# Norm, weight bounds and copies between the first output projection and the first feed-forward stage

## The chip, the cores and the metric

The kernel runs on one core of a Trainium2 chip. The metric is the device time in microseconds, the median of several runs of the whole program. The engines are named as in the profile: PE (matrix engine), PEld (its weight loads), DVE (VectorE), ACT (ScalarE), POOL (GpSimd) and SP (the engine that issues most of the loads).

## The reference

Two layers of a hybrid backbone work on 1024 latent tokens and 256 context tokens with 1024 channels. What matters here is the seam between the mixer of layer 0 and its feed-forward part:

```python
        h_lat = h_lat + g1 * y_lat
        h_lat = h_lat + g2 * swiglu(modulate(rms_norm(h_lat, norm2_g[i]), sh2, sc2),
                                    ffn_w_gate[i], ffn_w_up[i], ffn_w_down[i])
        if not last:
            h_ctx = h_ctx + cg1 * y_ctx
            h_ctx = h_ctx + cg2 * swiglu(modulate(rms_norm(h_ctx, norm2_g[i]), csh2, csc2),
                                         ffn_w_gate[i], ffn_w_up[i], ffn_w_down[i])

def swiglu(u, w_gate, w_up, w_down):
    return (jax.nn.silu(u @ w_gate) * (u @ w_up)) @ w_down
```

`y_lat` and `y_ctx` are the mixer's outputs, already multiplied by `w_out`. The feed-forward width is 2816, that is 22 blocks of 128.

## The kernel before, in words

**Layout.** Channels lie on the 128 partitions, tokens along the free axis. The tokens are in three column pieces: 0 and 1 are the two latent halves of 512, piece 2 is the context (256). A matrix product in fp32 precision is made of three products: each operand is split into a high part (a cast on ACT) and a low part (a subtraction on DVE, `split`, line 302, its cast line 300). `lin` multiplies one block of 128 output channels by all eight input blocks: 24 matmuls for each piece.

**Output projection** (`out_proj`). Two groups run one after the other: pieces (2, 0), then piece 1. Each group has eight blocks. A block's weights are fetched one block ahead through two pairs of buffers. After a block's matmuls, DVE adds the result to the residual `h` (line 1210), ACT squares the new `h` (line 509) and DVE adds the squares to an accumulator (line 514). After each block the generator `fill` is stepped once. At the end of a group `after1` is called. For group one it writes `h` to DRAM (POOL), computes the RMS factors (`rms`: one-column matmuls of the accumulator against ones, a square root and a reciprocal, matmuls that spread the result over the partitions, a copy), makes the context's normalized operand `uf` (lines 556 to 559), loads `h` of piece 1, and makes the first operands of the Strassen-Winograd products (`wino_first`). For group two it writes `h` and computes the factor, which is kept in `rest`.

**Bounds of weights.** Operands of the later half-precision products need scales. `qkv_sums` (the `fill` generator) loads 44 tiles of later weights, half a megabyte each, on POOL's queue, and ACT sums their absolute values (`abs_sums`, line 1264). It yields after every third tile. The first four tiles belong to the first feed-forward scales and are needed by `first_scales(0)` in `after1`; the other 40 are needed much later.

**Feed-forward, first stage** (`ffn`, layer 0). A loop over 22 blocks computes the context's hidden part: load and split gate and up weights, 24 matmuls of each, SiLU on ACT (line 1542), a product on DVE (line 1543), a store on POOL. From the third block on, each block steps the generator `second` (`wino_second`), which makes 20 of the operands for the latent half (line 1365 and what follows, casts at line 1358); they are held behind the previous block's last split on DVE. Then the Winograd stage begins: for each pair i of hidden blocks, gate and up products (`wino_steps`, matmuls at line 1462), with copies of the accumulator out of PSUM (`snap`, line 1467) between products that go on in the same accumulator. `fetch` loads the weights of the next product ahead and, where they have no scale yet, sums their absolute values.

**Order.** The program is written in source order, and the framework orders each engine's queue by planned times; an instruction earlier in the source goes first where both are ready. Engines run their queues in order. `follow(ins)` adds an order edge: the instructions in its block that run on the engine of `ins` are queued behind it. It adds no semaphore. Buffers come from pools: 20 of 4 KB (`S4`: tiles for the bounds, staging of gate and up weights, operands), 34 of 2 KB (`S2`), and so on.

## Time and profile before

| | |
|---|---|
| median of 3 runs | 2901.01 us (2895.24 to 2902.95) |
| profiled execution: its own time, its span | 2897.71 us, 2895.6 us |
| mean granted PE clock | 0.978 |
| output projection on PE | 718.2 to 839.1 us |
| context blocks of the feed-forward stage on PE | 845.1 to 975.3 us |
| Winograd stage on PE, from | 975.4 us |

In the tables by stretch, "10.20, 7.72 (x27)" is the stretch's length, then PE's busy time in it and the number of instructions recorded; the clock is the share of full speed that was granted to PE. In the timelines a row gives start, duration, engine, line, operation, tiles and shapes; the bracket at its end is how long the engine had been idle before it and what ended that. The names of tiles are the kernel's: `ps` and `pq` are accumulators in PSUM, `tk` holds squares, `wh` and `wl` the two parts of weights, `ws` and `s` staging buffers.

### The profile page before, as it was taken

The page shows a single profiled execution, that of the slowest core. Times are in us where ns is not written, and L with a number is a line of the kernel's source. Part 1 is how long each engine was busy: PE and PEld are TensorE (multiplying, and loading weights), DVE is VectorE, ACT ScalarE, POOL GpSimd, SP SyncE. Part 2 cuts the span into 40 slices and gives each one's busy share as a digit, 9 for nine tenths or more (in the row PEclk, how much of TensorE's full clock was granted, in tenths as well). Part 3 has the DMA queues.
Part 4 walks back from the last instruction along what each step waited for, and adds up shares of the span by engine and source line. Part 5 has one row for each costly group of instructions (what it writes and reads, how often), then busy time and mean ns, then how long its engine had stood idle before and what let it go on. Part 6 is the DMA issues. An engine that isn't in the chain of part 4 may idle for free. (4 is left out here: it accounts for less than half of the span.)

```text
span 2895.6 us, 46377 instructions
## 1 busy us (share of the span) xinstructions
PE 2758.4 (95%) x16419; PEld 1688.7 (58%) x16419; DVE 2081.9 (72%) x3857; ACT 1620.2 (56%) x2857; POOL 593.0 (20%) x977
## 2 busy tenths in 40 slices
PE   6989999999989999999999999999999899999998
PEld 3766557878879644444555844666664444444554
DVE  4778867585467798877886777777775778775755
ACT  4664325453675666654555555666663567554543
POOL 1012013354220111123120012343321112112000
PEclk8989999999999999999999999999999999999999
DMA  7574435358785655566995698777864756425753
GB/s 257 191 275 161 159 124 159 109 165 293 279 342 177 211 209 196 201 221 219 315 336 193 238 330 333 167 170 167 177 186 166 248 199 246 151 95 184 237 190 117
DMA packets 323363, 607.60 MB, mean 210 GB/s; under 512 B 89910, under 2 KB 131576, under 8 KB 323130
## 3 DMA queue, kind: packets, MB, share of 16 engines
q1 hardware_dynamic: 254682, 387.53, 41.6%
q0 software_dynamic: 66144, 212.91, 20.8%
q10 hardware_dynamic: 2304, 4.20, 0.4%
q8 instruction: 129, 2.11, 0.3%
q14 instruction: 104, 0.85, 0.1%
HBM read 455.33 MB, written 135.53 MB: 204 GB/s over the span
## 5 line engine op out<-in xcount | busy, mean ns | idle before, releaser
L1462 PE MATMUL ps<-s,s 128*128 128x512 f16 x2244 | 507.3, 381 | 8.9 <-ACT g L1467 4.7
L1462 PEld LDWEIGHTS <-s 128*128 128x128 f16 x2640 | 258.7, 98 | 332.3 <-issue 26.8
L296 PE MATMUL ps<-s,wh 128*128 128x256 f32 (+3 forms) x1764 | 402.3, 331 | 12.1 <-ACT wh L300 5.7
L1231 ACT ACTIVATE s<-s,c 128x512 f16<-128x512 f32 (+1 forms) x324 | 233.2, 752 | 147.3 <-DMA s<-d 71.4
L1232 DVE SCALAR_TENSOR_TENSOR s<-s,c,s 128x512 f16<-128x512 f32 (+1 forms) x324 | 247.3, 792 | 87.0 <-ACT s L1231 85.9
L1679 PE MATMUL ps<-s 128*128 128x512 f16 (+2 forms) x1308 | 303.8, 378 | 2.3 <-DVE s L1232 2.0
L296 PE MATMUL pq<-s,wh 128*128 128x512 f16 (+1 forms) x988 | 271.4, 352 | 5.0 <-DMA wh<-d 3.0
L296 PE MATMUL ps<-s,wl 128*128 128x256 f32 (+3 forms) x882 | 264.4, 332 | 2.6 <-DMA wl<-d 1.6
L1679 PEld LDWEIGHTS <-s 128*128 128x128 f16 x1536 | 148.4, 98 | 179.5 <-issue 7.4
L296 PEld LDWEIGHTS <-wh 128*128 128x128 f16 x1664 | 159.1, 99 | 151.1 <-issue 12.2
L287 POOL DMA_DIRECT2D d<-s x201 | 108.6, 541 | 652.2 <-DVE s L1523 186.1
L348 ACT CAST mat<-cs 128x1024 fp32r<-128x1024 f16 (+2 forms) x120 | 111.5, 934 | 140.5 <-PE ps L296 53.5
L296 PEld LDWEIGHTS ps<-s,wh 128*128 128x128 f32 x1088 | 178.3, 193 | 18.4 <-ACT wh L300 5.9
L296 PE MATMUL ps<-s,mat 128*128 128x512 f32 x696 | 183.1, 410 | 3.1 <-DVE s L302 2.8
L1462 PE MATMUL ps<-s,wh 128*128 128x512 f16 x608 | 182.3, 379 | 1.6 <-DVE g L1476 1.2
L296 PE MATMUL pq<-s,wl 128*128 128x512 f16 (+1 forms) x494 | 171.2, 352 | 0.0
L296 PEld LDWEIGHTS <-s 128*128 128x128 f16 x2400 | 113.6, 98 | 80.7 <-issue 12.8
L296 PEld LDWEIGHTS ps<-s,mat 128*128 128x128 f32 x696 | 135.7, 197 | 37.1 <-DVE s L302 3.2
L1264 ACT ACTIVATE t<-s 128x1024 bf16<-128x1024 f32 (+1 forms) x164 | 141.5, 864 | 13.4 <-DVE c L483 8.6
L296 PE MATMUL sc<-s,s 128*128 128x65 f16 (+3 forms) x2688 | 142.6, 231 | 3.2 <-ACT t L2080 2.4
L296 PEld LDWEIGHTS <-wl 128*128 128x128 f16 x832 | 81.8, 99 | 81.2 <-DMA wl<-d 2.5
L1231 ACT ACTIVATE s<-t,c 128x512 f16<-128x512 f32 x172 | 115.2, 712 | 21.9 <-DVE c L1330 9.3
(435 smaller groups left out, 5505.9 us busy)
## 6 DMA issues: line engine op xcount, KB each, us to landing
s<-d SPq DMA_DIRECT2D x294, 256.0 KB, 4.2
d<-s POOLq DMA_DIRECT2D x157, 256.0 KB, 3.7
s<-in_down SPq DMA_DIRECT2D x154, 256.0 KB, 5.0
s<-in_ada_w POOLq DMA_DIRECT2D x48, 512.0 KB, 4.9
s<-in_gate SPq DMA_DIRECT2D x46, 512.0 KB, 4.0
s<-in_up SPq DMA_DIRECT2D x46, 512.0 KB, 3.8
d<-g POOLq DMA_DIRECT2D x87, 256.0 KB, 3.4
d<-tk POOLq DMA_DIRECT2D x82, 256.0 KB, 4.9
```

What stands on the lines that cost most here:

```text
L287: self.last_ldr = self.nc.gpsimd.dma_start(out, in_).ins
L296: return self.nc.tensor.matmul(o, l, r, start=st, stop=sp).ins
L348: self.nc.scalar.copy(m, st)
L1231: nc.scalar.activation(hi, src, AF.Copy, scale=scale)
L1232: nc.vector.scalar_tensor_tensor(lo, src, scale, hi, op0=MUL, op1=SUB)
L1264: self.nc.scalar.activation(junk[:, :t.shape[1]], t, AF.Abs, scale=2.0 ** -15, accum_out=st[:, k:k + 1])
L1462: nc.tensor.matmul(ps, x[:, sl], y, start=first and j == 0 and x is wh and y is xh, stop=j == 3 and x is wl, skip_group_check=True)
L1679: m = nc.tensor.matmul(acc[j][:, c0:c1], x[:, sl], y[:, xs], start=first and k == 0, stop=last and k == 2, skip_group_check=True)
```

## The change

Four things are edited.

1. In `out_proj` the norm of a group is no longer computed at its end. `after1` writes `h` and loads the next `h`; a new function `norm1` (RMS factors, `uf`, scales, `wino_first`) is called in the next group, after the matmuls of its first block.
2. The factor of the second group is computed inside a new generator `second1`, so at the first step of `second`, in the third block of the feed-forward stage.
3. `qkv_sums` yields after every tile. Group one steps it three times for each block, group two once, and `ffn` gets the same generator as `fill` and steps it once a block from the third block on, draining it after the loop. These steps and `second` follow both the last split on DVE and the last cast on ACT of the previous block.
4. In layer 0 the `fetch` of the second pair's gate weights comes behind the first five steps of the first gate product, and `abs_sums` queues its sums from there on behind the last copy out of PSUM (`last_snap`).

```diff
-    def out_proj(self, wname, y, groups, h, l, m, after, fill):
+    def out_proj(self, wname, y, groups, h, l, m, after, norm, fill):
...
-        for pcs in groups:
+        for g, pcs in enumerate(groups):
             for nb in range(KB):
                 wh, wl = ready.pop(0)
                 fetch()
                 acc = self.lin(wh, wl, 0, range(KB), y, pcs)
-                next(fill, None)
+                if g and nb == 0:
+                    norm(groups[g - 1])
+                for _ in range(1 if g else 3):
+                    next(fill, None)
...
     def abs_sums(self, tiles, st):
 
         junk = self.T(BF16, 1024)
-        for k, t in enumerate(tiles):
-            self.nc.scalar.activation(junk[:, :t.shape[1]], t, AF.Abs, scale=2.0 ** -15, accum_out=st[:, k:k + 1])
+        with self.follow(self.behind):
+            for k, t in enumerate(tiles):
+                self.nc.scalar.activation(junk[:, :t.shape[1]], t, AF.Abs, scale=2.0 ** -15,
+                                          accum_out=st[:, k:k + 1])
...
             self.abs_sums([t], self.qs[:, k:k + 1])
-            if j % 3 == 2:
-                yield
-        yield
+            yield
...
         def snap(ps, tile=tile):
             t = tile()
-            nc.scalar.copy(t, ps)
+            self.last_snap = nc.scalar.copy(t, ps).ins
             return t
...
-                lo = self.last_lo
+                lo, hi = self.last_lo, self.last_hi
...
                 if fb >= 2:
-                    with self.follow(last):
+                    with self.follow(last[0]), self.follow(last[1]):
                         next(second, None)
-                last = lo
+                        next(fill, None)
+                last = lo, hi
+            for _ in fill:
+                pass
...
-            fetch(i + 1, 0)
+            if i or begun:
+                fetch(i + 1, 0)
             for k in (3, 4, 5) if i == 0 and l == 1 else ():
                 g.to(k)
                 up.to(k)
             g.to(5)
+            if i == 0 and not begun:
+                self.behind = self.last_snap
+                fetch(1, 0)
             up.to(1)
...
-        rest = []
-
         def after1(pcs):
             spill(h, hs0, pcs)
             if 0 in pcs:
-                uf.t.update(self.new_act(pcs=(2,)).t)
-                rs = self.rms(pcs)
-                for b in range(KB):
-                    self.norm_block({b: h.ap(0, b, 2)}, b, 2, 0, 3, uf, rs[0])
                 load_h((1,))
-                self.ucol, self.usi = self.operand_scale(0, 3, (0, 1))
-                self.first_scales(0)
-                for _ in self.wino_first(h, 0, 3, rs[1]):
-                    pass
-            else:
-                rest.append(self.rms((1,))[0])
+
+        def norm1(pcs):
+            uf.t.update(self.new_act(pcs=(2,)).t)
+            rs = self.rms(pcs)
+            for b in range(KB):
+                self.norm_block({b: h.ap(0, b, 2)}, b, 2, 0, 3, uf, rs[0])
+            self.ucol, self.usi = self.operand_scale(0, 3, (0, 1))
+            self.first_scales(0)
+            for _ in self.wino_first(h, 0, 3, rs[1]):
+                pass
+
+        def second1():
+            yield from self.wino_second(h, 0, 3, self.rms((1,))[0])
...
-        self.out_proj("w_out", y, [(2, 0), (1,)], h, 0, 2, after1, self.qkv_sums())
+        sums = self.qkv_sums()
+        self.out_proj("w_out", y, [(2, 0), (1,)], h, 0, 2, after1, norm1, sums)
...
-        self.ffn(0, uf, h3, hs0, (x for r in rest for x in self.wino_second(h, 0, 3, r)), after2, hd)
+        self.ffn(0, uf, h3, hs0, second1(), after2, hd, fill=sums)
```

## Prediction

> **What bounds the kernel now.** I read the page first, then the list of who waited for whom on the matmul engine around the change, then a table of busy time by stage, then the engines' timelines at each gap.

> ```profile
> PE 2758.4 (95%) x16419; PEld 1688.7 (58%) x16419; DVE 2081.9 (72%) x3857; ACT 1620.2 (56%) x2857; POOL 593.0 (20%) x977
> ```

> PE is busy for 95% of the span, so time can come from its gaps and from stretches in which its clock is not the full one. The stages of this change lie between 786 and 990 us. The next table gives, for each stretch, its length, the busy time of PE, PEld, DVE, ACT and POOL (with instructions), the granted clock, the DMA share and GB/s.

> ```profile
> 785.80:796.00 10.20, 7.72 (x27) 6.34 (x27) 7.06 (x19) 7.45 (x17) 1.08 (x2) 0.67 0.75 262
> 788.99:795.81 6.82, 6.82 (x21) 5.59 (x22) 3.82 (x14) 4.41 (x13) 0.00 (x0) 0.50 0.95 323
> 796.00:839.10 43.10, 43.10 (x185) 34.46 (x183) 29.80 (x44) 32.40 (x53) 13.78 (x26) 1.00 0.75 290
> 839.10:865.50 26.40, 21.12 (x155) 19.93 (x154) 11.20 (x15) 17.67 (x31) 2.17 (x4) 0.87 1.03 419
> 843.60:850.43 6.83, 4.82 (x21) 4.53 (x22) 2.78 (x3) 5.16 (x8) 0.42 (x1) 0.50 1.03 420
> 865.50:874.40 8.90, 5.37 (x24) 5.03 (x24) 7.88 (x11) 4.70 (x6) 0.54 (x1) 0.62 0.77 263
> 867.49:874.32 6.83, 5.24 (x23) 4.95 (x24) 5.81 (x8) 3.58 (x5) 0.00 (x0) 0.50 0.66 214
> 874.40:975.30 100.90, 100.90 (x891) 100.90 (x889) 74.34 (x93) 56.10 (x79) 10.25 (x19) 1.00 0.56 191
> 990.40:1257.00 266.60, 265.06 (x1241) 120.21 (x1240) 232.47 (x423) 175.30 (x333) 53.56 (x100) 1.00 0.57 202
> ```

> There are three boundaries at which PE falls short: the end of the projection's first group (786), the end of its second group (839), and between the third and the fourth feed-forward block (866). After each of them the granted clock is 0.50 for 6.8 us. A fourth gap, at 985, has no slow stretch behind it. PE's timeline names the releasers:

> ```profile
> 788.30 0.93 PE L296 MATMUL pq<-c,tk 128*128 128x1 f32 x5 [2.48 <-DVE tk L514]
> ...
> 841.51 1.05 PE L296 MATMUL pq<-c,tk 128*128 128x1 f32 x8 [2.23 <-DVE tk L514]
> 845.14 0.80 PE L296 MATMUL ps<-s,wh 128*128 128x256 f32 x2 [2.58 <-ACT wh L300]
> ...
> 868.61 0.79 PE L296 MATMUL ps<-s,wh 128*128 128x256 f32 x2 [3.07 <-ACT wh L300]
> ...
> 982.22 2.75 PE L1462 MATMUL ps<-s,s 128*128 128x512 f16 x12 [0.67 <-ACT g L1467]
> 987.83 0.38 PE L1462 MATMUL ps<-s,s 128*128 128x512 f16 x1 [2.86 <-ACT g L1467]
> ```

> Both first gaps (2.48 and 2.23) wait for the sum of squares of the last block (L514), and in both cases PE has nothing else in its queue ahead of that. The next two wait for a cast of weights on ACT, the last for the copy out of PSUM (L1467).

> **Part A: the norm a block later.** DVE's timeline at the first boundary:

> ```profile
> 785.64 1.14 DVE L1210 SCALAR_TENSOR_TENSOR s<-ps,c,s 128x256 f32<-128x256 f32 x2 [1.26 <-PE ps L296]
> 786.70 1.21 DVE L302 TENSOR_TENSOR wl<-ws,wh 128x1024 fp32r<-128x1024 f32 x1
> 787.83 1.02 DVE L514 TENSOR_TENSOR tk<-tk,tk 128x256 f32<-128x256 f32 x2
> ```

> The chain is eviction, a split of weights that happens to lie between, and the sums, which end at 788.8. After the change 24 matmuls of the second group's first block stand ahead of the sums' matmuls. Their weights are there: two pairs of buffers alternate, so the split at 786.70 is already that of the block after it. The 185 matmuls recorded in 43.10 us give 0.23 us each, so that block covers 24 x 0.23 = 5.6 us, more than the 2.48 that is missing. The 12 one-column matmuls and the ones that spread the result move and stay on PE, so they cost the same. The gain is the idle time 10.20 - 7.72 = 2.48 and half of the slow stretch, 6.82 / 2 = 3.41: 5.9 us.

> The cover can go: DVE is busy with the moved norm and the first operands just behind, 29.80 of 43.10 us, and the weights of the following blocks are split on the same queue. PE would run some 6 us ahead of where it is now, while this work starts about as late as before. If each lag falls on PE, all 5.9 is given back. More cannot be lost there, since PE would only wait for work that it waits for now. So A lies between 0 and 5.9. I take 5.9, because no gap in group two is recorded between 796 and 839 with the same work on DVE. Squares of the second group get in the queue behind the norm's, as now. The loads of h for the second group (eight on SP) are no longer behind the norm in program order; that is early, not late, and costs nothing.

> **Part B: the second group's sums go into the feed-forward stage, and 12 of the 44 weight tiles with them.** The ACT rows that end the second gap, the record of the summed tiles, and the issues of the gate weights:

> ```profile
> 844.06 1.03 ACT L300 CAST wh<-s 128x1024 fp32r<-128x1024 f32 x1
> 846.76 1.06 ACT L1264 ACTIVATE t<-s 128x1024 bf16<-128x1024 f32 x1 [1.67 <-DMA s<-in_gate]
> ```
> ```profile
> L1264 ACT ACTIVATE t<-s x44: 1039/1042/1057, 724.4 to 857.4; 128x1024 bf16<-128x1024 f32 x44
> ```
> ```profile
> L281 SPq DMA_DIRECT2D s<-in_gate x11: 327/328/328, 832.0 to 872.8; - x11
> ```

> The first gate block's weights are issued only at 832.0, behind the tiles for the bounds in the same pool of buffers, while the DMA engines are full (share 1.03, 419 GB/s). Then ACT, which works in order, stands 1.67 us at 846.76 for a bounds tile with a cast waiting behind it. The change leaves 24 tiles in group one (3 by 8, as before) and 8 instead of 20 in group two. The 12 others are 12 x 0.5 MB = 6 MB, which at 419 GB/s is 15 us of transfer taken from before the first gate weights. PE's queue then goes from the last projection block straight to the gate block, with no sum of squares between.

> The loss at this boundary is 26.40 - 21.12 = 5.28 idle, plus half of the 4.82 us that PE worked at half clock: 2.41, together 7.7. One pair of buffers for the up weights still comes free only when the last projection block ends. Its cast (1.03) and split (1.21 as at 786.70) take 2.2 us and the gate half of a block takes 24 x 0.113 = 2.7, so it just fits, with the last eviction and square on the same engines. I allow 1.0 for that. B lies between 0 (weights late anyway; below it only by the third rival) and 7.7; I take 6.7.

> The moved tiles cost ACT 12 x (1.04 + 0.19) = 14.8 us between the third and fourteenth block. The groups of ACT from 874 to 975 give the cover:

> ```profile
> L300 ACT CAST wh<-s 128x1024 fp32r<-128x1024 f32 x35 | 36.7, 1049 | 37.6 <-issue 26.2 <-PE ps L296 10.7 <-DMA s<-in_up 0.8
> L1358 ACT CAST s<-s 128x512 f16<-128x512 f32 x13 | 8.0, 615 | 1.1 <-DVE s L1379 0.9 <-DVE s L1371 0.2
> L1542 ACT ACTIVATE t<-ps 128x256 f32<-128x256 f32 x19 | 7.1, 374 | 0.0
> ```

> A block needs 2 x 1.05 + 0.62 + 0.37 = 3.1 us of ACT, with a tile 4.3; on PE it needs 48 matmuls at 100.90 / 891 = 0.113, that is 5.4. So 1.1 us a block is left, and the cost is zero as long as ACT does not stand. POOL issues the 12 loads among the stores of the hidden blocks, 0.5 us each, in a stage where it is busy for 10 of 101 us: zero.

> **Part C: follow also the cast.** The third gap on ACT:

> ```profile
> 859.70 1.28 ACT L1542 ACT_TABLE_LOAD   x1
> 861.00 0.66 ACT L1542 ACTIVATE t<-ps 128x256 f32<-128x256 f32 x2
> 862.03 0.38 ACT L1542 ACTIVATE t<-ps 128x256 f32<-128x256 f32 x1 [0.37 <-PE ps L296]
> 863.39 0.59 ACT L542 COPY t<-pq 128x512 f32<-128x512 f32 x1 [0.98 <-PE pq L296]
> 866.06 0.62 ACT L1358 CAST s<-s 128x512 f16<-128x512 f32 x1 [2.08 <-DVE s L1371]
> 866.99 0.62 ACT L1358 CAST s<-s 128x512 f16<-128x512 f32 x1 [0.31 <-DVE s L1371]
> 867.52 2.94 ACT L300 CAST wh<-s 128x1024 fp32r<-128x1024 f32 x3
> ```

> Three casts of weights wait behind the copy of the norm's factor and behind operands that DVE has not made yet. The loss is 8.90 - 5.37 = 3.53 idle and half of 5.24, together 6.2. The new order edge holds operands behind the previous block's casts; it adds no semaphore, only places in ACT's queue. But the chain from sums to factor to operand now starts here too, and its square root comes between two SiLUs. One row more of 1.28 on each side, 2.6 us in all, lies on ACT in the blocks where it is fullest. C lies between +6.2 and -2.6. With the loads no longer late the casts can stand earlier in the queue, against that stands the longer chain; I take half of the loss, 3.1.

> [...]

> **Part D: bounds behind the copy.** ACT ahead of the fourth gap:

> ```profile
> 986.18 1.04 ACT L1264 ACTIVATE t<-s 128x1024 bf16<-128x1024 f32 x1
> 987.12 0.19 ACT L1264 ACTIVATION_READ_ACCUMULATOR t<-s 128x1 f32 x1
> 987.22 0.56 ACT L1467 COPY g<-ps 128x512 f32<-128x512 f32 x1
> ```

> A bounds sum of the next gate weights holds up the copy that PE waits for; the copy by itself costs PE 0.67 (982.22). Behind the copy, the gap falls from 2.86 to 0.67: 2.2. The sums are 2.5 us later then, and their scale too; from 990.4 on PE has 265.06 of 266.60, so nothing there is late now. If PE waited for the later scale, 2.5 would be lost again and 0.3 more than gained. Two loads on SP move past the gate's products, which costs nothing while the buffers wait for the same splits. D lies between -0.3 and 2.2; I take 2.2.

> **Sum.** 5.9 + 6.7 + 3.1 + 2.2 = 17.9 us off the profiled execution's 2897.7 (span 2895.6 and 2.1 around it), which stands 3.3 under the median. Off the median of 2901.0 that is 2883. From 990 to 1257 DVE has 232.47 of 266.60, so a shift of the whole is not held back by another engine.

> **Rivals.** First, C turns bad: the chain and the tables push the casts later still. Then 5.9 + 6.7 + 2.2 - 2.6 = 12.2, 2889. For it speaks that three casts already queue there.

> Second, the feed-forward weights are late in any case, because their buffers come free no earlier than for the first issue at 832 now. B and C are 0, leaving 8.1: 2893. Against it stands the 6 MB less.

> Third, slower: ACT becomes the bound in the 12 blocks that got a tile, because it stands in order before each tile's landing with the casts behind it. Each block loses what this wait exceeds 1.1 us. With 14.8 gained elsewhere the gain is gone at 14.8 / 12 + 1.1 = 2.3 us a block; at 3.5 it is 12 x 2.4 - 14.8 = 14 slower, 2915. The one such wait on record is 1.67 at a DMA share of 1.03, and the stretch behind has 0.56.

> Fourth, the change does not do what it says: queues are ordered by the framework's planned times, and these may leave the sums' matmuls where they are. Then D alone acts, 2899.

> [...]

> **How the numbers follow.** The sum as forecast 0.56 (own range 2877 to 2889), the first rival 0.17, the second 0.14, the third 0.08, the fourth 0.05. What a measurement of this kernel can tell from no change is about 0.3%, 8.7 us: under 2892.3 is faster. Forecast and first rival give 0.73, second and fourth 0.19, third 0.08. All upper bounds together are 5.9 + 7.7 + 6.2 + 2.2 = 22.0, 2879; the runs shown differ by 7.7, so I go 4 further, to 2875. Upwards the range takes in the second and fourth rival, to 2900, and leaves out the third.

> **What would show it.** A: no wait for L514 ahead of one-column matmuls, full clock from 786 to the end of group two, which ends near 833. B: a gate issue well before 832, a first gate matmul within 1 us of the last projection matmul, and 32 summed tiles by then. C: no wait over 1 us for L300 in blocks three to five; three table loads there would speak for the first rival. D: no third wait above 1 us before L1467. Waits of ACT for s at L1264 over 1.1 us in many blocks would make it wrong.

## The result, and the profile after

| | before | after |
|---|---|---|
| median (range), 5 runs of each | 2901.01 us (2895.24 to 2902.95) | 2886.16 us (2880.07 to 2890.35) |
| ratio, 95% interval | | 0.9949 (0.9932 to 0.9966) |
| profiled execution, its span | 2897.71, 2895.6 us | 2886.16, 2883.8 us |
| mean granted PE clock | 0.978 | 0.980 |

The kernel is faster, by 0.5% here and by 0.22% (0.9978, 0.9968 to 0.9988) in a second measurement on another chip, told below. Both intervals leave out 1. The sizes differ, because stretches that the change doesn't touch scatter too: among the profiles of this study the time from the down projection to the end lay between 1509.7 and 1520.9 us with the same number of instructions on each engine. (In some of them a few dozen stand in another order; before and the six profiles in which the order is that of before still lie between 1515.1 and 1520.9.) So I read the parts from stage times. These repeat: the stage from the first projection matmul to the first Winograd matmul took 247.6 us in the profile of after and 247.7 in that of the second measurement.

The page's busy times of after:

```profile
PE 2753.0 (95%) x16419; PEld 1682.7 (58%) x16419; DVE 2081.7 (72%) x3857; ACT 1621.1 (56%) x2859; POOL 595.0 (21%) x977
```

Busy times by stage of the kernel before (length, then PE, PEld, DVE, ACT, POOL, granted clock, DMA share, GB/s). The first row is projection and context blocks, the second the Winograd stage:

```profile
718.20:975.40 257.20, 245.91 (x1661) 225.49 (x1660) 155.88 (x218) 159.10 (x257) 43.19 (x81) 0.96 0.70 263
975.40:1374.80 399.40, 389.41 (x1813) 175.91 (x1812) 334.35 (x605) 251.71 (x468) 83.86 (x156) 1.00 0.59 209
```

The same view of after:

```profile
721.00:968.60 247.60, 239.42 (x1660) 220.16 (x1658) 155.22 (x217) 160.39 (x259) 43.45 (x81) 0.99 0.75 273
968.60:1368.10 399.50, 390.68 (x1812) 176.24 (x1812) 334.67 (x606) 251.29 (x469) 84.28 (x156) 0.99 0.60 209
```

The first stage lost 9.6 us, the second nothing. PE runs the same matmuls (x16419 on the page, as before), yet its busy time in the first stage falls by 245.91 - 239.42 = 6.5 us: that is stretches at half clock that are gone (the granted clock of the stage is 0.99 instead of 0.96). Its idle time falls from 11.3 to 8.2, by 3.1. So two thirds of the gain came from the clock, one third from the gaps themselves.

The stretches of after that answer to those of before:

```profile
796.90:837.90 41.00, 40.48 (x173) 32.32 (x173) 33.23 (x55) 23.97 (x43) 7.49 (x14) 1.00 0.59 213
837.90:856.50 18.60, 17.86 (x154) 17.62 (x152) 7.78 (x11) 17.07 (x28) 1.62 (x3) 1.00 0.96 380
856.50:868.00 11.50, 6.03 (x26) 4.91 (x27) 9.27 (x12) 6.33 (x10) 2.66 (x5) 0.70 0.80 268
860.28:867.10 6.82, 4.00 (x17) 3.71 (x18) 6.45 (x9) 5.72 (x8) 0.00 (x0) 0.50 0.90 324
```

Three boundaries with a half-clock stretch have become one in this stage. PE goes through the end of group two (837.9) at full clock (1.00 from 796.90 to 856.50). What is left lies at 856 to 868. Who made PE wait, from 785 to 1010 us (total us, times, longest):

```profile
PE ps L297 <- ACT wh L301: 5.4, 2, 4.9
PE ps L1466 <- ACT tk L1471: 2.4, 1, 2.4
PE ps L297 <- DVE st L1317: 1.5, 1, 1.5
PE ps L1466 <- ACT g L1471: 1.3, 2, 0.7
PE pq L297 <- ACT t L539: 0.8, 1, 0.8
PE ps L297 <- DVE wl L303: 0.5, 1, 0.5
```

Lines stand one to five later than before (the cast L300 is L301, the split L302 is L303, the sums' L514 is L515, the bounds' L1264 is L1269, the copy L1467 is L1471). Both waits for the sums of squares are gone. In their place stand a wait for L1317 (the later scales), one longer wait for a cast, and the D wait, now named `tk` instead of `g`.

ACT's timeline at the wait for the cast:

```profile
850.13 1.28 ACT L1546 ACT_TABLE_LOAD   x1
851.43 0.66 ACT L1546 ACTIVATE t<-ps 128x256 f32<-128x256 f32 x2
852.10 1.28 ACT L528 ACT_TABLE_LOAD   x1
853.40 0.26 ACT L528 ACTIVATE st<-pq,c 128x4 f32<-128x4 f32 x1
853.68 1.28 ACT L1546 ACT_TABLE_LOAD   x1
854.98 0.38 ACT L1546 ACTIVATE t<-ps 128x256 f32<-128x256 f32 x1
...
857.74 0.59 ACT L543 COPY t<-pq 128x512 f32<-128x512 f32 x1 [1.22 <-PE pq L297]
860.40 1.22 ACT L1362 CAST s<-s 128x512 f16<-128x512 f32 x2 [2.08 <-DVE s L1375]
861.53 1.99 ACT L301 CAST wh<-s 128x1024 fp32r<-128x1024 f32 x2
```

The three table loads of the first rival are there. The two casts at 861.53 are for the next block's weights; they stand behind the copy of the factor and behind two operands, for which ACT waits 2.08 us. PE stands 4.93 us for them.

The gate issues, then the summed tiles of after:

```profile
L282 SPq DMA_DIRECT2D s<-in_gate x10: 327/328/430, 819.7 to 876.0; - x10
L1269 ACT ACTIVATE t<-s x44: 1041/1043/1057, 727.2 to 924.0; 128x1024 bf16<-128x1024 f32 x44
```

The first gate weights are issued at 819.7, not 832.0, and the sums run on to 924.0 instead of 857.4. At the end of group two 26 of the 44 are done (38 before), so 18 fall into the feed-forward stage.

### The profile page after: what moved, and what is told of

Same layout as the page of the kernel before. It is cut to its first block, busy times and chain, and to the rows that moved or that the text cites. A ratio compares the mean times of both kernels' runs of the same rounds, so it can differ in the third digit from the quotient of the medians.

```text
span 2883.8 us, 46373 instructions
## 1 busy us (share of the span) xinstructions
PE 2753.0 (95%) x16419; PEld 1682.7 (58%) x16419; DVE 2081.7 (72%) x3857; ACT 1621.1 (56%) x2859; POOL 595.0 (21%) x977
## 5 line engine op out<-in xcount | busy, mean ns | idle before, releaser
L297 PE MATMUL ps<-s,wh 128*128 128x256 f32 (+3 forms) x1764 | 399.2, 330 | 11.1 <-ACT wh L301 5.4
L1235 ACT ACTIVATE s<-s,c 128x512 f16<-128x512 f32 (+1 forms) x324 | 234.0, 753 | 148.6 <-DMA s<-d 82.0
L1236 DVE SCALAR_TENSOR_TENSOR s<-s,c,s 128x512 f16<-128x512 f32 (+1 forms) x324 | 248.2, 794 | 87.1 <-ACT s L1235 86.4
L1269 ACT ACTIVATE t<-s 128x1024 bf16<-128x1024 f32 (+1 forms) x164 | 141.6, 865 | 14.9 <-DVE c L484 9.4
L1235 ACT ACTIVATE s<-t,c 128x512 f16<-128x512 f32 x172 | 115.1, 712 | 21.1 <-DVE c L1334 11.3
```

What stands on the lines that cost most here:

```text
L297: return self.nc.tensor.matmul(o, l, r, start=st, stop=sp).ins
L1235: nc.scalar.activation(hi, src, AF.Copy, scale=scale)
L1236: nc.vector.scalar_tensor_tensor(lo, src, scale, hi, op0=MUL, op1=SUB)
L1269: self.nc.scalar.activation(junk[:, :t.shape[1]], t, AF.Abs, scale=2.0 ** -15, accum_out=st[:, k:k + 1])
```

## The experiments

The table comes first; all rows are read from the same places of each kernel's profile. S1 is the stage from the first projection matmul to the first Winograd matmul, S2 the stage from there to the first matmul of the down projection. Group two counts from the start of its first matmul to the start of its last, and the gate from the first matmul behind that. "Both" is S1 + S2 against before's 656.5, and beside it stands what the medians of the runs gave against the kernel before on the same chip.

| kernel | group two | to first gate matmul | gate to Winograd | S1 | S2 | both | medians | ratio, 95% |
|---|---|---|---|---|---|---|---|---|
| before | 53.4 | 6.3 | 130.2 | 257.1 | 399.4 | | | |
| after | 49.6 | 0.2 | 130.6 | 247.6 | 399.5 | -9.4 | -14.8 | 0.9949 (0.9932 to 0.9966) |
| after, again | 49.6 | 0.2 | 130.6 | 247.7 | 399.2 | -9.6 | -7.2 | 0.9978 (0.9968 to 0.9988) |
| A alone | 49.6 | 10.2 | 141.1 | 268.2 | 401.9 | +13.6 | +10.2 | 1.0037 (1.0023 to 1.0051) |
| tiles alone | 61.5 | 0.2 | 123.3 | 252.3 | 403.6 | -0.6 | +0.6 | 0.9999 (0.9988 to 1.0011) |
| after, tiles back | 51.2 | 9.1 | 142.8 | 270.3 | 401.6 | +15.4 | +15.0 | 1.0049 (1.0033 to 1.0065) |
| after, norm at end | 62.6 | 0.2 | 132.0 | 262.0 | 397.7 | +3.2 | +5.8 | 1.0007 (0.9992 to 1.0022) |
| after, factor at end | 51.2 | 0.2 | 129.6 | 248.2 | 399.6 | -8.7 | -11.2 | 0.9953 (0.9936 to 0.9970) |
| after, C's edge undone | 51.2 | 0.2 | 131.1 | 249.7 | 401.5 | -5.3 | -5.0 | 0.9980 (0.9968 to 0.9991) |
| after, casts ahead | 51.2 | 0.2 | 129.7 | 248.4 | 400.3 | -7.8 | -12.0 | 0.9960 (0.9946 to 0.9974) |
| after, D undone | 51.2 | 0.2 | 131.3 | 249.9 | 399.4 | -7.2 | -4.8 | 0.9977 (0.9965 to 0.9990) |
| after, scales later | 48.1 | 0.2 | 130.6 | 246.2 | 399.7 | -10.6 | -13.8 | 0.9948 (0.9934 to 0.9963) |
| all three | 48.1 | 0.2 | 123.9 | 239.5 | 399.5 | -17.5 | -18.6 | 0.9927 (0.9910 to 0.9943) |
| all three, D undone | 48.1 | 0.2 | 124.4 | 240.0 | 404.1 | -12.4 | -12.4 | 0.9955 (0.9940 to 0.9970) |

The two stages account for the medians within 5.4 us in every row, within 3 in nine of the thirteen. In "tiles alone" and "norm at end" two matmuls of the gate stand in PE's queue ahead of the rest of the last projection block; they are counted to group two here. Where an expectation speaks of a slow window, it means a stretch at half clock; the clock's window is the step of 3.413 us on which such stretches start (last section).

### The change once more

The same kernel, on another chip.

> The changed kernel once more, beside the version below. Both theories: the stretch from the projection to the Winograd stage 247.6 to 249.9 us, by the phase of the clock's window, the whole 8 to 20 us under the kernel before.

The median was 2887.18 against 2894.36. The stage repeats to 0.1 us (247.7), and so do the waits of 1.50, 0.81 and 4.93 us, to 0.01. The gain in the two stages is 9.6 us (9.4 in the first profile), and the two timings, 14.8 and 7.2, lie on both sides of it.

### The norm a block later, alone

Undone: the second factor in `second1`, the spread tiles, C's edge, D.

```diff
-                for _ in range(1 if g else 3):
+                for _ in range(3):
                     next(fill, None)
...
-            yield from self.wino_second(h, 0, 3, self.rms((1,))[0])
+            yield from self.wino_second(h, 0, 3, rest[0])
```

> The kernel before with part A alone: the first group's norm one block later, the loads of the second group's h ahead of it; tiles for the bounds, the second factor and the sums of the second pair's weights as before, steps behind the split alone. Theory (A stands by itself and is worth the first gap less 1.5): group two from first to last matmul 49.6 or 51.2 us (slow window), then the second gap and the late weights as before; the stretch from the projection to the Winograd stage 253 to 255.5 us against 257.1. Rival (A does not stand by itself: with 20 tiles in group two, the tiles' transfers, started later behind the later norm, push the first gate weights out): 258 us or more, as the kernel with the tiles back had 270.3.

A alone makes the kernel 10.2 us slower, though group two itself is as short as in after (49.6). PE's waits from 785 to 990 us:

```profile
PE ps L297 <- ACT wh L301: 11.0, 3, 5.6
PE pq L297 <- ACT t L539: 7.5, 1, 7.5
PE pq L297 <- DVE tk L515: 3.2, 1, 3.2
```

What A gains in group two, 3.8 us, is lost almost four times over behind it: 3.9 up to the first gate matmul and 10.9 from there on. The loads of the 20 tiles of group two begin later on POOL, at 824.5 us instead of 809.6, and then fall where the first gate weights should load: the first of those is issued at 836.4 instead of 832.0. That the first operands, made a block later, hold the buffers for the tiles is argued from the code; the rows show only that POOL waits for ACT. POOL's timeline of A alone:

```profile
824.53 2.12 POOL L288 DMA_DIRECT2D s<-in_wk  x4 [2.56 <-ACT wh L301]
```

And of before:

```profile
809.59 1.58 POOL L287 DMA_DIRECT2D s<-in_wk  x3
```

In after the same loads begin as late (827.2, 39.0 us behind the first matmul of group two, as here), but there are only 8 of them.

### The spread tiles, alone

Undone: the norm's move, the factor's move, D. Kept: one tile a block in group two, the rest in the feed-forward stage, and C's edge.

```diff
             after(pcs)
+            if not g:
+                norm(pcs)
...
-                if g and nb == 0:
-                    norm(groups[g - 1])
```

> The kernel before with the moved bounds tiles alone: 24 in group one, 8 in group two, 12 in the feed-forward stage; norm and second factor at the ends of their groups, the second pair's sums early. Theory (tiles alone bring the gate weights, but the projection's own weights of group two suffer as they did in the kernel with the norm at the end): the first gap of 2.5 us as before, waits of 2 to 3 us for casts in group two, the stretch 254 to 262 us. Rival (the tiles are all of part B whatever the norm does): 250 to 252 us.

PE's waits from 785 to 990 us:

```profile
PE ps L297 <- ACT wh L301: 4.9, 2, 2.4
PE pq L297 <- DVE tk L515: 2.5, 1, 2.5
```

The wait for the first group's sums stays (2.5), that of the second group is gone, and so is the one at the third block. S1 falls by 4.8, and the time moves inside it. Group two is 8.1 us longer than before (61.5 against 53.4), with two waits of 2.4 us for casts of the projection's own weights. From its end on S1 is 13.0 shorter (0.2 and 123.3 against 6.3 and 130.2), and PE is busy for 121.85 us of those 123.3 (in "all three" it is 122.68 of 123.90, at a granted clock of 1.00): the third gap is not there. But the ratio is 0.9999, since S2 is 4.2 longer. That is taken up under D.

Alone, the two give +11.1 and -4.8 in S1; together with C and D they give -9.5. They are not terms of a sum.

### All of the change but the spread tiles

```diff
-                for _ in range(1 if g else 3):
+                for _ in range(3):
```

> The changed kernel, but all 44 tiles for the bounds are stepped in the output projection again (three a block in both groups, none left for the feed-forward stage). Theory 1 (12 tiles fewer ahead of the gate weights bring those in time): the first gate weights are issued after 830 us again, and the matmul engine waits 2 to 6 us for the first cast at the start of the feed-forward stage; the stretch from the projection to the Winograd stage grows by 3 to 8 us. Rival (the moved tiles matter little, the factor's new place did it): the stretch stays within 1 us of 247.6.

One edit turns 9.5 us of gain in S1 into 13.2 of loss, more than either theory allowed. PE's waits from 785 to 1000 us:

```profile
PE ps L297 <- ACT wh L301: 10.3, 3, 4.9
PE pq L297 <- ACT t L539: 9.8, 1, 9.8
PE pq L297 <- DVE tk L515: 2.7, 1, 2.7
```

ACT's timeline of the same kernel around them:

```profile
867.30 1.06 ACT L1269 ACTIVATE t<-s 128x1024 bf16<-128x1024 f32 x1 [2.81 <-DMA s<-in_up]
...
869.80 1.06 ACT L1269 ACTIVATE t<-s 128x1024 bf16<-128x1024 f32 x1 [1.35 <-DMA s<-in_up]
...
873.06 1.28 ACT L539 ACTIVATE t<-c,st 128x128 f32<-128x128 f32 x4
```

ACT stands in order before tiles that have not landed, and the factor's four multiplications at 873.06, for which PE waits 9.8 us, stand behind them. This is the mechanism of the prediction's third rival, in the place from which the change takes it away. The sums of squares, too, are back in front of the first gate matmul (844.29), although the source computes the factor only in the third block:

```profile
838.30 1.05 PE L297 MATMUL pq<-c,tk 128*128 128x1 f32 x8 [2.68 <-DVE tk L515]
```

### All of the change but the norm's move

```diff
             after(pcs)
+            if not g:
+                norm(pcs)
...
-                if g and nb == 0:
-                    norm(groups[g - 1])
```

> The changed kernel, but the norm of the first group is computed at the end of that group again. Theory 1 (part A is the wait for the last squares and the half clock behind it, less what was given back): the wait of 2.5 us for the sums and a slow stretch of 6.8 us return at the end of group one, and the 1.5 us wait for the bounds' sum in block two of the second group goes; group two from its first to its last matmul 53 to 54 us against 49.6 now, the whole 3.8 slower. Rival (the first gap is covered by other work either way): the stretch is within 1 us.

S1 is 262.0, 14.4 longer than in after, of which 13.0 lie in group two (62.6 against 49.6) and 1.4 behind it (132.0 against 130.6). The whole is within the measurement of the kernel before. With the norm at the end, the spread tiles and the factor in the third block together are worth less than the tiles alone (252.3): the parts need one another in both directions. One of its delays, on ACT's timeline:

```profile
833.78 1.04 ACT L301 CAST wh<-ws 128x1024 fp32r<-128x1024 f32 x1 [3.56 <-DMA ws<-in_w_out]
```

The projection's own weights land late, and PE stands 2.70 us for this cast. The loads on SP show a reason: here the last two loads of projection weights are issued at 819.4 and 823.6, behind four loads of gate and up weights at 814.7 to 816.3, and in "tiles alone" it is likewise (822.6 and 826.6, behind 817.9 to 819.6); in after the last one is issued at 819.3, ahead of the first gate load at 819.7. No run changes that order by itself.

### The factor at the end of group two

The second factor is computed where it was; all else as in after.

```diff
             if 0 in pcs:
                 load_h((1,))
+            else:
+                rest.append(self.rms((1,))[0])
...
-            yield from self.wino_second(h, 0, 3, self.rms((1,))[0])
+            yield from self.wino_second(h, 0, 3, rest[0])
```

> The changed kernel, but the second group's RMS factor is computed at the end of the output projection again. [...] From the first projection matmul to the first Winograd matmul 246 to 253 us (changed kernel 247.6, before 257.1). Rival (the factor's place is all of part B): the stretch returns by the whole 6.0 us, to 253 or more.

There is no wait at the boundary here either: 0.2 us to the first gate matmul (839.33). The sums do not stand in front of it, though the source has them there; the framework queues them behind 55 feed-forward matmuls:

```profile
845.72 0.95 PE L297 MATMUL pq<-c,tk 128*128 128x1 f32 x8
```

In "tiles alone" they stand behind gate matmuls as well, in "tiles back" and "A alone" in front of them. So the factor's place in the source is not what took the gap away: with 8 tiles in group two, and early gate weights, the queue has gate matmuls ahead of the sums; with 20 it has not. From gate to Winograd it is 1.0 us shorter (129.6 against 130.6), so moving the factor costs 1.0. The third gap stays all the same: PE waits 4.2 us for the cast, with one table load there instead of three.

### C's new edge undone

```diff
-                    with self.follow(last[0]), self.follow(last[1]):
+                    with self.follow(last[0]):
```

> The changed kernel, but the operand steps follow only the last split on DVE, not also the last cast on ACT. Theory 1 (the order edge to the cast is inert where the third gap lies: the casts that wait there are those of the next block, and the edge is to the block before): the wait of 4.9 us for the casts and the three table loads stay, the stretch from the projection to the Winograd stage is within 1 us of the changed kernel's but for a slow window of the clock (1.7 us). As predicted (the edge is worth half of the third gap's loss): about 3 us slower.

The queues of PE, DVE and POOL are the same, operation by operation and tile by tile, that of ACT up to 933 us, and the wait for the cast is the same 4.9. The edge to the previous block's cast changes nothing at the place it was costed for. The ratio differs from the first one of after, but the difference of 2.1 us in S1 is 1.6 in group two (below, under the clock) and 0.5 behind it. S2 is 2.0 longer too, which stays unexplained.

### Casts of the next block ahead of the factor

Weights are fetched one block ahead, and the chain of the factor is queued behind the next block's casts.

```diff
+            ws = block(0)
             for fb in range(NFB):
+                (gh, gl), (uh, ul) = ws
...
+                if fb < NFB - 1:
+                    ws = block(fb + 1)
                 if fb >= 2:
-                    with self.follow(last[0]), self.follow(last[1]):
+                    with self.follow(self.last_lo), self.follow(self.last_hi):
```

> The changed kernel, but each feed-forward block's weights are loaded, cast and split in program order ahead of the previous block's operand step, and the operand and bounds steps follow the split and the cast of the block ahead. Theory 1 (the third gap is ACT's queue: the casts of the fourth block stand behind the factor's copy and the first operands): the 4.9 us wait falls to 0 to 2 us although three table loads stay, and the stretch to the Winograd stage is 4 to 8 us shorter, 240 to 244. Rival (the table loads and the chain's length are what the matmul engine waits for): the wait stays above 3 us at the same or the next block.

PE's waits from 838 to 969 us:

```profile
PE ps L297 <- ACT wh L301: 2.4, 2, 2.1
PE ps L297 <- DVE wl L303: 1.5, 2, 0.8
```

The longest wait falls from 4.9 to 2.1 and the wait for the factor is gone, with the three table loads still there. So the casts' place in ACT's queue makes the larger part of the 4.9 in this kernel. But little of it is gained: the stretch from gate to Winograd is 0.9 shorter (129.7 against 130.6), not the 4 to 8 expected. PE's idle time there falls from 6.2 to 3.9, and a half-clock stretch of 6.83 us stays, in which PE now works 6.13 us instead of 4.00.

### D undone

```diff
-            if i or begun:
-                fetch(i + 1, 0)
+            fetch(i + 1, 0)
...
-            if i == 0 and not begun:
-                self.behind = self.last_snap
-                fetch(1, 0)
```

> The changed kernel, but the weights of the second pair are fetched ahead of the first gate product again and their sums are free to run ahead of the copies. Theory as predicted (part D is worth 2.2): 2.2 us slower, with the 2.9 us wait for the third copy back. Rival (the wait was only moved, from the first gate product's copy to one of the up product's at 1006 us): the stretch from the first Winograd matmul to the down stage stays at 399 us within 1, the 2.9 us wait returns at its old place and the 2.4 us one goes.

S2 is 399.4, as in after (399.5). PE's timeline at 992 us:

```profile
992.42 2.75 PE L1466 MATMUL ps<-s,s 128*128 128x512 f16 x12 [2.87 <-ACT g L1471]
```

The old wait is back where it was. In after it is at another place, as ACT's timeline there shows:

```profile
1004.35 1.04 ACT L1269 ACTIVATE t<-s 128x1024 bf16<-128x1024 f32 x1
...
1005.39 0.71 ACT L1235 ACTIVATE s<-t,c 128x512 f16<-128x512 f32 x1
1006.00 0.56 ACT L1471 COPY tk<-ps 128x512 f32<-128x512 f32 x1
```

A later copy waits behind a bounds sum of other weights and an operand (L1235), and PE stands 2.41 us for it at 1006.62. PE's timeline in after:

```profile
979.86 2.75 PE L1466 MATMUL ps<-s,s 128*128 128x512 f16 x12 [0.67 <-ACT g L1471]
...
1006.62 4.44 PE L1466 MATMUL ps<-s,s 128*128 128x512 f16 x12 [2.41 <-ACT tk L1471]
```

Twelve matmuls take 4.44 us behind this wait instead of 2.75: it also costs clock (0.50 from 1007.05 to 1010.46), which the old wait did not (in before 1.00 from 987.83 to 1000). So the wait moved to another copy; it was not taken away. This is not all there is to D. In the pair of "all three" with and without D, S2 is 399.5 and 404.1, in "tiles alone" without it 403.6. With D, S2 lay between 397.7 and 401.6 in all nine profiles; without it, between 399.4 and 404.1 in five. So D is worth nothing in after, and 4.6 between the two kernels of "all three". What decides between them stays open.

### The scales of the first gate product later

In after PE stands 1.50 us behind the first group for a small matmul of `first_scales` (L1317), which needs a reduction that DVE does only behind an eviction, a split of weights and a reciprocal that waits for a square root on ACT. Here `first_scales(0)` is called at the end of group two.

```diff
             self.ucol, self.usi = self.operand_scale(0, 3, (0, 1))
-            self.first_scales(0)
...
             if 0 in pcs:
                 load_h((1,))
+            else:
+                self.first_scales(0)
```

> The changed kernel, but the first feed-forward scales (a one-column sum over partitions on the matmul engine) are computed at the end of the second group and not in the norm. Theory 1 (what is left of the first gap is this matmul: it stands in the matmul engine's queue for 1.5 us behind a reduction that DVE does after a split): the 1.5 us wait goes, group two takes 48 to 48.5 us against 49.6 without a slow window and 51.2 with one. Rival (the spreading matmuls behind it would wait as long for ACT): a wait of 1 us or more in the same place on the square root's factor.

Group two takes 48.1 us, 1.5 less, and stands at full clock (1.00 from 785 to 836). Nothing else in S1 moves.

### All three together

Scales later, casts ahead, and the factor's chain started in the first context block ahead of its SiLU, so that the square root needs no load of its own between two SiLUs (ACT's rows from 842 to 870 have one table load here, 1.28 us at 851.66, where after has three).

```diff
                 ua = self.lin(uh, ul, 0, range(KB), u, (2,))[2]
+                if fb == 0:
+                    next(second)
...
-            yield from self.wino_second(h, 0, 3, self.rms((1,))[0])
+            r = self.rms((1,))[0]
+            yield
+            yield from self.wino_second(h, 0, 3, r)
```

> The changed kernel with three moves: the second group's factor in the first feed-forward block (one table load instead of three), the casts of the next block ahead of the operand steps, and the first scales at the end of the second group. Theory 1: no wait over 1 us from the first projection matmul to the Winograd stage; that stretch is 237 to 241 us against 247.6, and the whole kernel 7 to 10 us faster than the changed one. Rival (the wait moves on to the operands: the Winograd stage waits for operands that come a block later): the gain is given back behind the stretch, above 399.5 us from there to the down stage.

The table by stretch, the whole of S1 and the part from the end of group two:

```profile
720.80:960.20 239.40, 237.71 (x1660) 218.59 (x1658) 153.48 (x214) 155.18 (x254) 44.23 (x82) 1.00 0.78 283
836.30:960.20 123.90, 122.68 (x1067) 121.59 (x1066) 89.38 (x112) 85.31 (x133) 18.96 (x35) 1.00 0.81 286
```

PE's waits from 785 to 1010 us:

```profile
PE ps L297 <- ACT wh L301: 0.9, 2, 0.5
PE ps L297 <- DVE wl L303: 0.8, 1, 0.8
PE ps L1466 <- ACT g L1471: 0.7, 1, 0.7
```

PE is busy for 122.68 of 123.90 us at full clock (1.00). At 2877.07 us this kernel beats both: 0.9927 (0.9910 to 0.9943) of before. Its S1 is 8.2 us shorter than that of after: 6.5 of idle time (8.2 to 1.7) and 1.7 of PE's busy time (239.42 to 237.71), which is about what the last half-clock stretch cost (4.00 / 2 = 2.0). Alone, the later scales gave 1.5 and the casts ahead 0.9 of it; the earlier chain was not run by itself.

### All three, D undone

The edit is that of "D undone", on top of the last kernel.

> The version with the three moves, and the second pair's bounds early again as in the kernel before. Theory (part D moves a wait and is worth nothing): the stretch to the Winograd stage 239 to 241 us, the one behind it 398 to 401, the whole 7 to 10 us under the changed kernel beside it. Rival (D's 2.2 us are real where the stage ahead does not hide them): the stretch behind it 401 to 402.

2881.97 us, 0.9955. S1 is the same within 0.5, S2 4.6 longer, more than either expectation. From 960 to 1364 PE has 5.9 us of waits for the copy `g` where the kernel with D has 0.7; all its waits there are 12.8 us against 8.7:

```profile
PE ps L1466 <- ACT g L1471: 5.9, 4, 2.9
```

## Why the prediction was right in its total and wrong in its parts

The forecast was 2883 us (own range 2877 to 2889, 2875 to 2900 with the rivals), and 2886.2 was measured. That total holds. In the second measurement the kernel before stood at 2894.4, so 17.9 less would have been 2876.5, and 2887.2 was measured: there the gain was 7.2. The sum of 17.9 does not hold by its parts: the two stages gave 9.5. By its own steps:

| step | taken (bounds) | measured | from |
|---|---|---|---|
| A | 5.9 (0 to 5.9) | 3.8 | group two 53.4 to 49.6 |
| B | 6.7 (0 to 7.7) | 7.7 | no half clock from 837.9 on and no wait up to that for the factor at 856.6 |
| C | 3.1 (-2.6 to 6.2) | -2.0 | 6.2 lost before; 6.2 idle and 4.00 / 2 of half clock after |
| D | 2.2 (-0.3 to 2.2) | 0 | S2 399.4 and 399.5 |
| sum | 17.9 | 9.5 | |

**A: right mechanism, size too large.** The wait for L514 is gone and the clock is full to the end of group two, as listed. The failed step is "the gain is the idle time 10.20 - 7.72 = 2.48": behind the sums stood a second chain in the same call, through the scales, with a reduction on DVE that lies behind an eviction and a split. Its 1.50 us, and 0.5 more for a cast of weights later in the group, replaced most of the 2.48. "Scales later" shows this: 48.1, which makes A's gain 5.3.

**B: right size, half the cause.** The gate issue came early (819.7), the first gate matmul follows within 0.23 us, and the boundary runs at full clock (1.00 from 837.90 to 856.50). But I counted on two edits, the sums moved away and the weights early. "Factor at end" shows that the tiles and their early weights are enough, and "tiles back" that the factor's new place in the source does not move the sums without them. That is the lever of the fourth rival, queues ordered by planned times, though its outcome did not come. The count was off: 26 tiles at that point, not 32, since I counted steps of the generator, and ACT had not yet made the sums of the last six. ACT bore 18 tiles instead of 12, and it had the room:

A group of ACT in after, from 874 to 975 us (busy us, mean ns, then idle time before it):

```profile
L1269 ACT ACTIVATE t<-s 128x1024 bf16<-128x1024 f32 x10 | 10.5, 1050 | 0.0
```

ACT never stands before a tile there, nor between 838 and 874. The third rival did not happen at its place.

**C: wrong sign; the first rival's step.** I took half of the loss as gained, since "the casts can stand earlier in the queue". They did not: an order edge behind the previous block's cast does nothing here ("C's edge undone"), and the casts still stand behind the copy of the factor and the first operands. The rival's price, -2.6 for two rows of 1.28, was near the measured -2.0, and its three table loads are there. But the loads are not the larger cause: with them and the casts ahead the wait is 2.1 instead of 4.9. Nor does the chain explain it all: with the chain back at the end of group two and one load ("factor at end") the stretch is 1.0 shorter, half of the 2.0, and the wait is still 4.2, where before had 3.07. So the price was near in part by luck, and what makes the other half was not isolated. "Tiles alone", in which PE comes to this stage later, has no such gap; that would fit a PE that now runs ahead of ACT and DVE, but it is not shown.

**D: wrong.** The sentence "so nothing there is late now" was read from PE's busy time in the old order; the failed step is that the copies behind were taken to be free. One of them met the next sum.

**What the sum lacked altogether** is that A and B depend on one another. I gave A a low bound of 0, "PE would only wait for work that it waits for now". A alone is 11.1 us slower in S1, and the rows show POOL's tile loads delayed into the next stage's weights. With the other parts in place the same A is worth 14.4 (262.0 against 247.6). That cover, the tiles moved away, was not named.

That the total came out near is partly luck. The errors of A, C and D all went one way, 9.4 us too much less the 1.0 too little of B, and the first timing hid 5.4 of these 8.4, since it gave that much more than the stages account for. The second did not.

## What to carry to other kernels

Engines worked their queues in order here (in "tiles back" ACT stood 2.81 and 1.35 us before tiles that had not landed, and PE 9.8 us for what was queued behind them), so work that is made early for a later stage belongs behind the casts and copies that PE needs next; look at who stands behind a waiting instruction before pricing the wait. Look, too, where the framework has put a moved step: its place in the source need not be its place in the queue. When a step is moved later, follow the buffers that it takes: the prefetch behind it moves too, and two edits that each look like a gain can cost one by one and pay only together. Read a small change from the length of its stage and the half-clock rows; the total of this kernel scatters by more than the parts.

## What the runs showed of the hardware

The same 1.50 us wait of PE behind group one was followed by a half-clock stretch in some kernels and by none in others. In after, the 10 us from that wait's end:

```profile
796.90:806.90 10.00, 9.96 (x42) 7.84 (x42) 4.47 (x12) 6.20 (x16) 0.54 (x1) 1.00 0.19 68
```

The first 3.4 us behind the same wait in "factor at end":

```profile
796.60:800.00 3.40, 3.36 (x9) 2.69 (x9) 0.51 (x4) 2.15 (x8) 0.00 (x0) 0.51 0.53 171
```

It costs 1.6 us in group two (51.2 against 49.6) in five of the eight kernels that have this wait, though PE, DVE, ACT and POOL have done the same instructions up to it in all eight. Half-clock stretches here last 3.41 us (796.66 to 800.07 in "factor at end") or 6.83 (860.28 to 867.11 in after), and up to 17.07 where PE waits longest ("tiles back"). The 2.86 us wait in before had none behind it, a 1.50 us one here had.

On ACT a table load takes 1.28 us, and the next activation starts 0.02 us behind its end (850.13 to 851.43, 852.10 to 853.40, 853.68 to 854.98). In before it is the same: the load at 859.70 takes 1.28, and SiLU starts at 861.00.
